# The front of a hybrid encoder layer: keys and values of the attention projected last and kept on chip, queries first

## The chip, the core and the metric

One of the eight cores of a Trainium2 chip runs the kernel. Its engines work side by side and wait for each other by semaphores: PE (TensorE: matmuls and transposes, results into PSUM), DVE (VectorE), ACT (ScalarE), POOL (GpSimd) and SP (SyncE, which here only issues transfers, as POOL does too). The metric is the time of one execution on the device in microseconds (us), the median of several runs.

## What is computed

The layer works on x of 1024 tokens by 1024 channels in fp32. After a LayerNorm one projection of 2048 columns is split into retention (queries, keys, values, gate of 256 each), an S5 branch (256), and windowed attention (512 of queries, 128 of keys, 128 of values). The three results are joined, projected out, added to the residual, normed, and followed by an expert layer of 16 experts and a last norm:

```
proj = jnp.einsum('bld,de->ble', h, w_in[l])
rq, rk, rv, rg, su, aq, ak, av = jnp.split(proj, _split_points(), axis=-1)
...
kb = jnp.concatenate([kp[:, :-2], kp[:, 1:-1], kp[:, 2:]], axis=2)
...
scores = jnp.einsum('bcqkgd,bcskd->bckgqs', qb, kb).astype(f32)
...
scores = scores - slopes * jnp.abs(rel).astype(f32)
...
m = jnp.maximum(jnp.max(scores, axis=-1, keepdims=True), sink_f)
p = jnp.exp(scores - m)
denom = jnp.sum(p, axis=-1, keepdims=True) + jnp.exp(sink_f - m)
probs = (p / denom).astype(v.dtype)
out = jnp.einsum('bckgqs,bcskd->bcqkgd', probs, vb)
...
h = layer_norm(DEEPNORM_ALPHA * h + mix, ln1_g[l], ln1_b[l])
ffn = expert_choice_ffn(h, router_w[l], exp_w_gate[l], exp_w_up[l], exp_w_down[l])
```

Each block of 128 queries sees its own and both neighbouring blocks of keys; eight query heads share two heads of keys and values.

## The kernel before

Products in fp32 are made of three matmuls: each operand is split into a high part (ScalarE copies it) and the remainder (VectorE subtracts), and high x high, low x high and high x low are summed in PSUM (lines 74 to 76). Weights come in pieces of 1 MB as raw tiles (tag wraw, pool raw, two slots; `Units.load`, line 121) and are split half by half into tiles whl (lines 125 and 130).

The program up to about 305 us is `front()`. Its pieces are put with `at(place, fn)` at places, numbers that are sorted once; the program of every engine follows that order. Each engine works its instructions off in order. The string `order` (line 1165) sets the middle of it: K0, K1 and V0, V1 are the halves (512 tokens) of the attention's keys and values, q00 to q31 the four pieces of 128 columns of queries by half, g0 to g7 the gates and r0 to r7 the outputs of the eight chunks of the retention, and o0 to o3 the four output products of S5 (lines 807 and 810). WA holds the weights of keys and values, W6 and W7 those of the queries, WG those of the gate. Between them run the S5 lags (class Lags, lines 718 to 761): matmuls at line 739, copied by ScalarE into a tile KC (lines 749, 751), which lies in the pool raw with tag wraw too, and stored from there by POOL in eight transfers m_d (line 761).

Keys, before: the PSUM rows of a half are split into a tile kst (lines 849 and 858) and stored to DRAM (line 861). Values: they are copied (line 866), turned by four transposes, split into kst and stored (line 887). Queries: kst (lines 851 and 893), stored four times for each piece (q_d, line 899). Near the end of the front, POOL loads KHL (keys, 64 channels of high part twice over and remainders) and AV (values) from DRAM (lines 1294, 1296) into the space of the split weights, and the queries of a step as qs (line 1285; a ring of three).

Attention has 16 steps i, two to a block of 128 tokens. `attention_scores` takes four heads: two matmuls each (lines 1326, 1327), and VectorE adds the bias and takes the maximum while it writes a score row S (line 1329; rows in a ring of 12; the small statistics asm in a ring of 4). `attention_exp` is ScalarE's exponential (line 1345), `attention_out` scales, transposes (line 1364) and multiplies with AV (po, line 1371). From step 2 on the steps stand in a loop in which a scheduler of the tile framework orders the instructions; output projection (lines 74 to 76 with WO), statistics (z, lines 1406 and 1493) and the router run in the same loop, each some steps behind. Ahead of the loop, the front ends with the S5 gate: YG (line 814), transposes (line 822), gate matmuls (line 828), glu and YO (lines 836 to 838), with hb, half of the gate's bias (line 781). The experts follow at about 520 us.

## Time and profile before

| | |
|---|---|
| median of 3 runs | 1681.29 us (1679.31 to 1686.14) |
| the profiled execution | 1684.39 us |
| its span in the profile | 1682.7 us |
| TensorE busy | 1601.5 us (95%) |
| VectorE busy | 1413.9 us (84%) |
| ScalarE busy | 1126.2 us (67%) |
| GpSimd busy | 209.4 us (12%) |

The profile gives times from the span's start. An entry of the timeline is start, duration, engine, line and operation; in brackets stands how long the engine was idle just before, and what ended that. PEclk is the granted clock of TensorE as a share of full speed. Matmuls overlap each other, so their cost is the distance of their starts, not the duration of one.

### The profile page before, as it was taken

How to read it: one execution, taken by the hardware profiler on the slowest of the kernel's cores; microseconds unless marked ns; L12 is line 12 of the kernel's file. 1: busy time of each engine (PE TensorE's matmuls, PEld its weight loads, DVE VectorE, ACT ScalarE, POOL GpSimd, SP SyncE). 2: the span in 40 equal slices, each digit the busy share in tenths (PEclk: the TensorE clock that was granted, in tenths of full speed). 3: DMA queues.
4: the chain of work that ended last, by engine and by line, in shares of the span. 5: the costliest groups of instructions: out<-in, count | busy, mean ns of one | idle time of the engine just before them, and what ended most of it. 6: DMA issues, size and time to landing. Idle time of an engine off the chain costs nothing.

```text
span 1682.7 us, 21145 instructions
## 1 busy us (share of the span) xinstructions
PE 1601.5 (95%) x7704; PEld 1294.4 (77%) x7704; DVE 1413.9 (84%) x1728; ACT 1126.2 (67%) x1266; POOL 209.4 (12%) x243
## 2 busy tenths in 40 slices
PE   6998998799898999999999999999999999999997
PEld 4886887477776788888888888888887787778785
DVE  7984872677788999998988988889888999989996
ACT  4644463666654677777777777777777777877773
POOL 3001211101101010101101011010111213221221
PEclk9998999899999999999999999999999999999998
DMA  4564478714316899999999999999999999999993
GB/s 181 190 165 128 132 206 254 215 49 140 95 63 258 307 386 384 408 379 383 365 392 368 366 398 354 386 374 382 386 364 407 397 395 382 382 410 385 397 418 139
DMA packets 104986, 512.03 MB, mean 304 GB/s; under 512 B 13233, under 2 KB 28337, under 8 KB 54194
## 3 DMA queue, kind: packets, MB, share of 16 engines
q1 hardware_dynamic: 88354, 479.75, 74.7%
q0 software_dynamic: 16528, 30.94, 6.6%
q8 instruction: 60, 0.98, 0.2%
q14 instruction: 44, 0.36, 0.1%
HBM read 464.50 MB, written 46.14 MB: 303 GB/s over the span
## 4 chain that ended last, share of the span: by engine, by line
PE 59%; DVE 16%; DMA 10%; issue 8%; ACT 6%; POOL 1%; SPq 0%; POOLq 0%; DVEq 0%; ACTq 0%
PE gu L1827 26%; PE y L1827 13%; DVE whl L1874 6%; PE mm L74 4%; PE mm L76 4%; PE mm L75 4%; DMA zz<-acc_d 3%; DMA wraw<-in_exp_w_gate 3%; ACT whl L1867 2%; DMA wraw<-in_exp_w_down 2%; PE tp L1812 2%; PE po L1371 1%; ACT S L1345 1%; DMA wraw<-in_exp_w_up 1%; DMA qs<-q_d 1%
## 5 line engine op out<-in xcount | busy, mean ns | idle before, releaser
L1874 DVE TENSOR_TENSOR whl<-wraw,whl 128x2048 fp32r<-128x2048 f32 x384 | 873.3, 2289 | 95.0 <-ACT whl L1867 94.5
L1867 ACT ACTIVATE whl<-wraw 128x2048 fp32r<-128x2048 f32 x384 | 734.6, 1917 | 245.7 <-PE gu L1827 86.7
L1827 PE MATMUL gu<-whl,xT 128*128 128x512 f32 x3072 | 741.0, 398 | 0.0
L1827 PEld LDWEIGHTS gu<-whl,xT 128*128 128x128 f32 x3072 | 571.3, 189 | 124.7
L1827 PE MATMUL y<-whl,hT 128*128 128x512 f32 x1536 | 368.7, 395 | 0.7 <-ACT hT L65 0.7
L1827 PEld LDWEIGHTS y<-whl,hT 128*128 128x128 f32 x1536 | 288.6, 188 | 69.5 <-ACT hT L65 0.9
L1801 POOL DMA_INDIRECT xs<-h_d,index x15 | 41.4, 2758 | 738.5 <-PE y L1827 490.0
L74 PE MATMUL mm<-hT,whl 128*128 128x512 f32 x160 | 65.8, 412 | 0.0
L65 ACT ACTIVATE hT<-tp 128x512 fp32r<-128x512 f32 x80 | 45.9, 583 | 28.7 <-PE tp L1812 14.4
L76 PE MATMUL mm<-hT,whl 128*128 128x512 f32 x160 | 63.0, 394 | 0.0
L75 PE MATMUL mm<-hT,whl 128*128 128x512 f32 x160 | 62.6, 391 | 0.0
L66 DVE TENSOR_TENSOR hT<-tp,hT 128x512 fp32r<-128x512 f32 x80 | 54.1, 684 | 9.2 <-ACT hT L65 9.1
L74 PE MATMUL mm<-WO,yh 128*128 128x512 f32 x128 | 53.2, 415 | 4.7 <-ACT yh L65 4.7
L1812 PE MATMUL tp<-ident,hid 128*128 128x128 f32 x256 | 39.4, 277 | 14.3 <-DVE hid L1909 14.3
L75 PE MATMUL mm<-WO,yh 128*128 128x512 f32 x128 | 52.1, 407 | 0.0
L1812 PEld LDWEIGHTS tp<-ident,hid 128*128 128x128 f32 x256 | 31.3, 141 | 25.9 <-DVE hid L1909 18.8
L1329 DVE CUSTOM_DVE_ANT_0 S<-at,R,sink 128x384 f32<-128x384 f32 (+1 forms) x64 | 35.8, 581 | 17.3 <-PE tp L1364 11.7
L76 PE MATMUL mm<-WO,yl 128*128 128x512 f32 x128 | 50.3, 403 | 0.0
L74 PE MATMUL mm<-whl,hT 128*128 128x512 f32 (+1 forms) x128 | 46.8, 366 | 1.5 <-ACT hT L65 1.4
L1345 ACT ACTIVATE S<-S,asm 128x384 f32<-128x384 f32 (+1 forms) x64 | 36.9, 577 | 14.1 <-DVE asm L1332 13.9
L76 PE MATMUL mm<-whl,hT 128*128 128x512 f32 (+1 forms) x128 | 44.4, 347 | 1.2 <-DVE hT L66 1.2
L75 PE MATMUL mm<-whl,hT 128*128 128x512 f32 (+1 forms) x128 | 44.4, 347 | 1.1 <-DVE whl L130 1.1
(430 smaller groups left out, 1792.3 us busy)
## 6 DMA issues: line engine op xcount, KB each, us to landing
wraw<-in_exp_w_gate SPq DMA_DIRECT2D x128, 1024.0 KB, 7.7
wraw<-in_exp_w_up SPq DMA_DIRECT2D x128, 1024.0 KB, 8.1
wraw<-in_exp_w_down SPq DMA_DIRECT2D x128, 1024.0 KB, 8.0
wraw<-in_w_in SPq DMA_DIRECT2D x8, 1024.0 KB, 7.2
x<-in_x SPq DMA_DIRECT2D x8, 512.0 KB, 4.6
h_d<-x SPq DMA_DIRECT2D x8, 512.0 KB, 3.2
q_d<-kst SPq DMA_DIRECT2D x32, 128.0 KB, 4.8
wraw<-in_w_out SPq DMA_DIRECT2D x4, 1024.0 KB, 6.4
```

The source lines that it names most:

```text
L65: nc.scalar.activation(hi, src, AF.Copy)
L66: eng.tensor_tensor(lo, src, hi.bitcast(F32), OP.subtract)
L74: nc.tensor.matmul(ps, a[0], b[0], start=start, stop=False)
L75: nc.tensor.matmul(ps, a[0], b[1], start=False, stop=False)
L76: nc.tensor.matmul(ps, a[1], b[0], start=False, stop=stop)
L1329: nc.vector.tensor_tensor_reduce(s[:, :W], ps[:, :W], K.R[:, ro:ro + W], 2.0 ** -(h + 1), K.sink[:, h:h + 1], OP.add, OP.max, accum_out=m[ ...
L1345: nc.scalar.activation(S[g][:, :W], S[g][:, :W], AF.Exp, bias=nm[:, g:g + 1], accum_out=rs[:, g:g + 1])
L1801: nc.gpsimd.indirect_dma_start(out=xs, out_offset=None, in_=K.h1_dram, in_offset=bass.IndirectOffsetOnAxis(ap=K.index[:, e:e + 1], axis=0))
L1812: K.nc.tensor.transpose(pt[:, c, :], src[:, (c0 + c) * P:(c0 + c + 1) * P], K.ident)
L1827: nc.tensor.matmul(ps, a[s][c], u[:, t, i * w:(i + 1) * w], start=first and id(ps) not in began, stop=last and left[id(ps)] == 0)
L1867: self.K.nc.scalar.activation(u[:, 0, :], self.raw[k1].rearrange("p a b -> p (a b)"), AF.Copy)
L1874: self.K.nc.vector.tensor_tensor(u[:, 1, :], raw, u[:, 0, :].bitcast(F32), OP.subtract)
```

## The change

Queries are projected first and keys and values last: the string `order` is new, W6 takes the early load of WA, W7 is loaded next and WA last. Keys and values are not stored to DRAM and loaded again: their PSUM rows are split where they lie into the tiles KHL and AV, for keys in pieces of 64 rows, with two copies for the second 64 rows. That takes out eight stores and four loads of keys and two and two of values.

For the space, the pool of split weights becomes two pools. The one of side 1 is closed when the retention is done (`keys_space`), and KHL and AV are put there. The last two tiles of side 0 become the score rows (`attention_space`), ten in place of twelve; the statistics asm come from another pool, three in place of four.

The scores of steps 0 and 1 are issued ahead of and among the S5 gate instead of behind it. At the start of the kernel, the small chain `ops[0:14]` (rsmall) moves ahead of the second norm, the split of WK[1] behind it, and the second part of the first projection to a later place. The diff, cut to its core:

```diff
-        u = self.K.hl.tile([P, 2, 1024], F32R, name="whl", tag=f"whl{self.side}", bufs=2)
+        u = self.K.hl[self.side].tile([P, 2, 1024], F32R, name="whl", tag="whl", bufs=2)
...
-def key_rows(K, parts, half):
-
-    ks = parts[0]
-    K.nc.vector.tensor_tensor(ks[:, 1], parts[1].ps, ks[:, 0].bitcast(F32), OP.subtract)
+def key_rows(K, p, half):
+
+    nc, hs = K.nc, slice(half * 512, (half + 1) * 512)
+    a, b = slice(0, 64), slice(64, P)
     for kv in range(2):
-        for r in range(2):
-            K.nc.sync.dma_start(K.k_dram[half][kv][r * 64:(r + 1) * 64], ks[kv * 64:(kv + 1) * 64].bitcast(F32))
+        split(K, K.KHL[kv][a, 0, hs], K.KHL[kv][a, 1, hs], p.ps[kv * 64:(kv + 1) * 64])
+    for kv in range(2):
+        nc.scalar.activation(K.KHL[kv][b, 0, hs], K.KHL[kv][a, 0, hs].bitcast(F32), AF.Copy)
+        nc.vector.tensor_copy(K.KHL[kv][b, 1, hs], K.KHL[kv][a, 1, hs].bitcast(F32))
...
-def value_high(K, pt):
-    vs = K.ast.tile([P, 4, 2, 2, 64], F32R, name="kst", tag="k4", bufs=3)
...
-def value_parts(K, parts, half):
-    vs, pt = parts
-    K.nc.vector.tensor_tensor(vs[:, :, :, 1], pt, vs[:, :, :, 0].bitcast(F32), OP.subtract)
-    K.nc.sync.dma_start(K.v_dram[half], vs.bitcast(F32))
+def value_parts(K, pt, half):
+    av = K.AV[:, half * 4:half * 4 + 4]
+    split(K, av[:, :, :, 0], av[:, :, :, 1], pt.rearrange("p b (k c) -> p b k c", k=2))
...
+    spread(9.95, 0.001, ops[0:5])
...
-    at(10.3, lambda: WK[1].high(0))
-    at(10.4, lambda: WK[1].high(1))
-    at(10.5, lambda: WK[1].low(0))
-    at(10.6, lambda: WK[1].low(1))
+    spread(10.3, 0.01, ops[5:14])
     at(11.0, norm[1].gain)
     at(11.1, norm[1].shift)
-    spread(11.2, 0.001, ops[0:5])
-    spread(11.3, 0.01, ops[5:14])
+    at(11.2, lambda: WK[1].high(0))
+    at(11.3, lambda: WK[1].high(1))
+    at(11.4, lambda: WK[1].low(0))
+    at(11.5, lambda: WK[1].low(1))
...
-        at(s + 6.2 if t else 11.8, lambda p=p, c=6 if t else 4: p.part(c, 8))
+        at(s + 6.2, lambda p=p, c=6 if t else 4: p.part(c, 8))
...
-    at(B + 2.0, WA.load)
+    at(B + 2.0, W6.load)
...
-    order = "K0 g0 g1 K1 r0 V0 r1 g2 r2 g3 V1 r3 q00 g4 r4 g5 q10 r5 g6 r6 q01 g7 r7 q11 q20 q30 o0 o1 q21 o2 q31 o3".split()
+    order = "q00 g0 g1 q01 r0 q10 r1 g2 r2 g3 q11 r3 q20 g4 r4 g5 q21 r5 g6 r6 q30 g7 r7 q31 V0 o0 K0 o1 V1 o2 K1 o3".split()
...
-    at(E0 + 1.5, lambda: WA.high(0))
+    at(E0 + 1.5, lambda: W6.high(0))
...
-    for wt, place, prev in ((W6, V0 + 4, ("K1", "V1")), (W7, V0 + 21, ("q01", "q11"))):
+    for wt, place, prev in ((W7, V0 + 15, (("q01", 0), ("q11", 1))), (WA, V0 + 21, (("q21", 1), ("q31", 0)))):
         at(place, wt.load)
...
-    at(R, lambda: close(X["retB"][0], K.c_ret))
+
+    def keys_space():
+        close(X["retB"][0], K.c_ret, K.c_hl1)
+        X["kv"] = pool("kv", side="right")
+        K.KHL = [X["kv"][1].tile([P, 2, L], F32R, name=f"KHL{kv}") for kv in range(2)]
+        K.AV = X["kv"][1].tile([P, NT, 2, 2, 64], F32R, name="AV")
+    at(R, keys_space)
...
-    def keys():
-        close(K.c_hl)
-        X["kv"] = pool("kv", side="right")
-        K.kv = X["kv"][1]
-        attention_keys(K)
-        X["at2"] = pool("at2", side="right")
-        K.at2 = X["at2"][1]
-    at(where["q31"] + 5.7, keys)
...
-        at(where["q21"] + 6.0 + i * 0.1, lambda i=i: attention_queries(K, i))
+        at(where["K1"] + 1.0 + i * 0.1, lambda i=i: attention_queries(K, i))
+    at(where["K1"] + 5.7, lambda: attention_space(K))
     for i in range(2):
-        at(G + 10.3 + i * 2.6, lambda i=i: attention_scores(K, i))
-        at(G + 12.9 + i * 2.6, lambda i=i: attention_exp(K, i))
+        at(G - 0.2 + i * 1.1, lambda i=i: attention_scores(K, i))
+        at(G + 10.4 + i * 2.6, lambda i=i: attention_exp(K, i))
...
+def attention_space(K):
+
+    t = [K.hl[0].tile([P, 2, 1024], F32, name="S", tag="whl", bufs=2).rearrange("p a b -> p (a b)") for _ in range(2)]
+    K.score = [t[i // 5][:, i % 5 * 3 * P:(i % 5 + 1) * 3 * P] for i in range(10)]
+    K.heads = 0
...
-    sm = K.at2.tile([P, 6, 4], F32, name="asm", bufs=4)
+    sm = K.small.tile([P, 5, 4], F32, name="asm", bufs=3)
...
-        s = K.at2.tile([P, 3 * P], F32, name="S", bufs=12)
+        s = K.score[K.heads % 10]
+        K.heads += 1
```

Three places of the program, in the order of each engine. First ScalarE, at the second KC of the S5 lags (at is the PSUM tile it copies, QT and qfb are retention's queries, kst the first projected piece of keys before, of queries after). Before:

```order
L340 ACTIVATE QT_165<-mm_1481 128x512
L751 ACTIVATE KC_1509<-at_1537 16x4x112 [waits PE_49]
L751 ACTIVATE KC_1509<-at_1571 16x4x112 [waits PE_49]
L749 ACTIVATE KC_1633<-at_1616 16x4x128 [waits DMASW3_49,DMASW2_49,DMASW4_49,DMASW1_49,DMASW5_49,DMASW0_49,DMASW6_49,DVE_49,DMASW7_49,PE_49,Activation_49]
L370 ACTIVATE qfb_1635<-QT_165 64x2x128 [waits DMAHW3_49]
L370 ACTIVATE qfb_1635<-QT_165 64x2x128 x3
L849 ACTIVATE kst_1661<-mm_1553 128x512 [waits DMAHW3_49,DMAHW4_49,DMAHW2_49,DMAHW5_49,DMAHW1_49,DMAHW7_49,DMAHW0_49,PE_49]
```

After:

```order
L340 ACTIVATE QT_162<-mm_1478 128x512
L751 ACTIVATE KC_1506<-at_1534 16x4x112 [waits PE_49]
L751 ACTIVATE KC_1506<-at_1568 16x4x112 [waits PE_49]
L749 ACTIVATE KC_1628<-at_1613 16x4x128 [waits DVE_49,PE_49,Activation_49]
L370 ACTIVATE qfb_1630<-QT_162 64x2x128 [waits DMAHW3_49]
L370 ACTIVATE qfb_1630<-QT_162 64x2x128 x3
L848 ACTIVATE kst_1656<-mm_1550,qscale_1327 128x512 [waits DMAHW3_49,DMAHW2_49,DMAHW4_49,DMAHW1_49,DMAHW5_49,DMAHW0_49,DMAHW7_49,PE_49,Pool_49]
```

The order of these rows is the same, but the second KC no longer waits for the transfers issued by POOL (DMASW). Beside it, SP's queue in the same stretch. Before, the load of a raw tile (wraw, W6) stood ahead of the stores of the first piece:

```order
L731 DMA BX_1629<-bx_d01_82 128x64 [waits DMAHW0_49,DVE_49]
L121 DMA wraw_1631<-in_w_in 128x2048 [waits Activation_49]
L861 DMA k_d00_103<-kst_1661 64x1024 [waits DMAHW1_49,DVE_49,Activation_49]
L861 DMA k_d00_103<-kst_1661 64x1024 [waits DMAHW2_49]
L861 DMA k_d01_104<-kst_1661 64x1024 [waits DMAHW3_49]
L861 DMA k_d01_104<-kst_1661 64x1024 [waits DMAHW4_49]
```

After, with the loads of retention's states (kv) behind those stores:

```order
L890 DMA q_d0_0_75<-kst_1656 64x512 [waits DMAHW2_49]
L890 DMA q_d0_0_75<-kst_1656 64x512 [waits DMAHW3_49]
L351 DMA kv_1698<-kv_d1_96 128x512 [waits DMAHW4_49]
L351 DMA kv_1793<-kv_d2_97 128x512 [waits DMAHW5_49]
L121 DMA wraw_1796<-in_w_in 128x2048 [waits DMASW5_49,DMASW4_49,DMASW6_49,DMASW3_49,DMASW7_49,DMASW2_49,DMAHW6_49,DMASW1_49,DMASW0_49]
L890 DMA q_d1_0_77<-kst_1819 64x512 [waits DMAHW7_49,Activation_49]
```

W6's load is gone from here, and W7's load, behind the first stores and two loads of kv, now has the wait for the transfers that POOL issued. The second place is VectorE at hb, at the end of the retention (whl is the last split weight, WO the output projection's). Before:

```order
L893 SCALAR_TENSOR_TENSOR kst_2780<-mm_2725,qscale_1330,kst_2780 128x512 [waits DMAHW4_49,Activation_49]
L130 TENSOR_TENSOR whl_2782<-wraw_1877,whl_2782 128x1024 [waits PE_49,Activation_49]
L781 TENSOR_SCALAR hb_2836<-bg_2834 128x2 [waits DMAHW2_49,DMAHW3_49,DMAHW1_49,DMAHW5_49,DVE_49,DMAHW6_49,PE_49,Activation_49]
L893 SCALAR_TENSOR_TENSOR kst_2821<-mm_2760,qscale_1330,kst_2821 128x512 [waits DMAHW7_49,DMAHW0_49]
L893 SCALAR_TENSOR_TENSOR kst_2880<-mm_2811,qscale_1330,kst_2880 128x512 [waits DMAHW6_49,DMAHW5_49,DMAHW7_49,DMAHW4_49,Activation_49]
L66 TENSOR_TENSOR WO1_2911<-wraw_2573,WO0_2910 128x1024 [waits PE_49,Activation_49]
L66 TENSOR_TENSOR WO1_2911<-wraw_2573,WO0_2910 128x1024 [waits Activation_49]
```

After:

```order
L884 SCALAR_TENSOR_TENSOR kst_2769<-mm_2714,qscale_1327,kst_2769 128x512 [waits DMAHW2_49,Activation_49]
L130 TENSOR_TENSOR whl_2771<-wraw_1874,whl_2771 128x1024 [waits PE_49,Activation_49]
L781 TENSOR_SCALAR hb_2835<-bg_2833 128x2 [waits DMAHW1_49,DMAHW3_49,DMAHW0_49,DMAHW4_49,DVE_49,DMAHW7_49,PE_49,Activation_49]
L66 TENSOR_TENSOR AV_2826<-tp_2846,AV_2826 128x8x64 [waits Activation_49]
L66 TENSOR_TENSOR KHL0_2824<-mm_2863,KHL0_2824 64x512 [waits Activation_49]
L66 TENSOR_TENSOR KHL1_2825<-mm_2863,KHL1_2825 64x512 [waits Activation_49]
L860 CAST KHL0_2824<-KHL0_2824 64x512 [waits DVE_49]
L860 CAST KHL1_2825<-KHL1_2825 64x512 [waits DVE_49]
```

The rows of queries behind hb are gone, and splits into AV and KHL stand there. The third place is TensorE behind the last S5 output (o3). Before, with the first scores behind all sixteen gate matmuls:

```order
L822 MATMUL tp_3055<-ident_128,YG_2831 128x128 x3
L822 MATMUL tp_3061<-ident_128,YG_2831 128x128 [waits PE_49]
L822 MATMUL tp_3061<-ident_128,YG_2831 128x128 x3
L828 MATMUL mm_3073<-yT_2984,wg_2832 128x512 [waits DVE_49]
L828 MATMUL mm_3073<-yT_2984,wg_2832 128x512 [waits Activation_49]
L828 MATMUL mm_3081<-yT_2984,wg_2832 128x512 [waits PE_49]
L828 MATMUL mm_3081<-yT_2984,wg_2832 128x512
L828 MATMUL mm_3092<-yT_2984,wg_2832 128x512 [waits Activation_49]
L828 MATMUL mm_3092<-yT_2984,wg_2832 128x512
L828 MATMUL mm_3099<-yT_2984,wg_2832 128x512 [waits Activation_49]
L828 MATMUL mm_3099<-yT_2984,wg_2832 128x512
L1326 MATMUL at_3107<-KHL0_3037,qs_2962 128x256 [waits DMASW3_49,DMASW0_49]
```

After:

```order
L1310 MATMUL at_3052<-KHL0_2824,qs_2979 128x256 [waits DVE_49]
L1311 MATMUL at_3052<-KHL0_2824,qs_2979 128x256
L1310 MATMUL at_3056<-KHL0_2824,qs_2979 128x256 [waits DVE_49]
L1311 MATMUL at_3056<-KHL0_2824,qs_2979 128x256
L822 MATMUL tp_3062<-ident_122,YG_2830 128x128 [waits Activation_49]
L822 MATMUL tp_3062<-ident_122,YG_2830 128x128 x3
L822 MATMUL tp_3068<-ident_122,YG_2830 128x128 [waits PE_49]
L822 MATMUL tp_3068<-ident_122,YG_2830 128x128 x3
L1310 MATMUL at_3075<-KHL1_2825,qs_2981 128x256 [waits DMASW1_49,DVE_49]
L1311 MATMUL at_3075<-KHL1_2825,qs_2981 128x256
```

The scores (at, line 1310) of step 0 now stand ahead of the transposes of YG, and those of step 1 between them and the gate.

## Rows read from the trace of the kernel before

**Rows 1.** Busy time of the engines (with the number of instructions) in three stretches: the S5 output, the head of attention, the experts; then the granted clock of TensorE, the DMA engines' share, GB/s.

```profile
250.00:291.00 41.00, 36.47 (x206) 32.13 (x205) 9.73 (x11) 12.69 (x18) 3.90 (x6) 0.92 0.85 257
291.00:346.00 55.00, 41.94 (x155) 28.89 (x156) 34.77 (x96) 38.05 (x93) 6.65 (x15) 0.84 0.63 189
...
700.00:1682.00 982.00, 959.90 (x4374) 776.12 (x4372) 876.19 (x578) 721.38 (x529) 129.88 (x77) 0.99 0.96 375
```

**Rows 2.** Waits of TensorE from 0 to 305 us, by line and releaser: total in us, times, the longest.

```profile
PE at L739 <- ACT KC L749: 6.6, 1, 6.6
...
PE mm L807 <- DVE kst L893: 4.5, 1, 4.5
PE tp L173 <- DVE x L164: 4.1, 2, 2.6
```

**Rows 3.** The same from 291 to 540 us.

```profile
PE at L1326 <- DMA qs<-q_d: 5.3, 1, 5.3
PE mm L74 <- ACT yh L65: 4.7, 3, 3.5
```

**Rows 4.** Timeline of all engines from 148 to 167 us, at the two KC tiles: start, duration, engine, line.

```profile
149.55 0.42 SPq L121 DMA_DIRECT2D wraw<-in_w_in  x1
...
149.86 4.50 POOL L761 DMA_DIRECT2D m_d<-KC  x8 [22.99 <-DVE stmp L314]
...
150.04 1.05 PE L739 MATMUL at<-WO,BX 128*16 128x128 f32 x8
...
151.01 0.39 PE L74 MATMUL mm<-whl,hT 128*128 128x256 f32 x1
...
152.38 0.28 PE L76 MATMUL mm<-whl,hT 128*128 128x256 f32 x1
...
158.64 0.59 ACT L749 ACTIVATE KC<-at 16x512 f32<-16x512 f32 x1 [12.81 <-DMA m_d<-KC]
...
159.28 1.89 PE L739 MATMUL at<-WO,BX 128*16 128x128 f32 x8 [6.62 <-ACT KC L749]
...
161.10 0.58 PE L74 MATMUL mm<-whl,hT 128*128 128x256 f32 x1
...
163.96 1.77 PE L739 MATMUL at<-WO,BX 128*16 128x128 f32 x8
```

**Rows 5.** Timeline of ScalarE and of SP behind it, at the second split weight and the loads of kv; and from the list of transfers, the loads of the input weights (number, size, us from issue to landing).

```profile
175.69 1.06 ACT L125 ACTIVATE whl<-wraw 128x1024 fp32r<-128x1024 f32 x1
...
183.24 1.29 ACT L416 ACTIVATE ro<-po,rnm,rrs 128x64 f32<-128x64 f32 x4 [4.74 <-DVE rnm L413]
...
166.36 2.32 SPq L351 DMA_DIRECT2D kv<-kv_d  x2
...
wraw<-in_w_in SPq DMA_DIRECT2D x8, 1024.0 KB, 7.2
```

**Rows 6.** Timeline of TensorE in the start, at the transposes of the second token tile.

```profile
22.42 1.07 PE L173 MATMUL tp<-ident,x 128*128 128x128 f32 x8 [0.98 <-DVE rsmall L259]
```

**Rows 7.** Timeline of SP, VectorE and TensorE from 261 to 290 us, the S5 output products.

```profile
261.36 0.43 SPq L777 DMA_DIRECT2D bg<-in_ssm_b_glu  x1
...
264.21 0.17 DVE L781 TENSOR_SCALAR hb<-bg 128x2 f32<-128x2 f32 x1 [9.77 <-DMA bg<-in_ssm_b_glu]
...
265.13 0.80 PE L807 MATMUL mm<-MU 128*128 128x128 f32 x2 [4.51 <-DVE kst L893]
...
266.57 0.64 PE L807 MATMUL mm<-MU 128*128 128x128 f32 x2
...
267.85 0.64 PE L807 MATMUL mm<-MU 128*128 128x128 f32 x2
...
288.80 0.39 PE L807 MATMUL mm<-MU 128*128 128x128 f32 x2
...
289.47 0.39 PE L807 MATMUL mm<-MU 128*128 128x128 f32 x2
```

**Rows 8.** Instructions by line and shape up to 520 us, splits of 64 and of 128 rows: busy time, mean ns of one, idle time ahead.

```profile
L66 DVE TENSOR_TENSOR yl<-po,yh 64x512 fp32r<-64x512 f32 x16 | 10.9, 680 | 4.2 <-ACT yh L65 3.9
...
L65 ACT ACTIVATE yh<-po 64x512 fp32r<-64x512 f32 x16 | 9.4, 587 | 7.5 <-PE po L1371 7.3
...
L858 DVE TENSOR_TENSOR kst<-mm,kst 128x512 fp32r<-128x512 f32 x2 | 1.4, 676 | 0.0
```

**Rows 9.** Timeline of all engines from the last S5 output to the first statistic.

```profile
291.01 0.60 ACT L814 ACTIVATE YG<-mm 128x512 f32<-128x512 f32 x1 [1.99 <-PE mm L810]
...
305.04 0.39 PE L1326 MATMUL at<-KHL,qs 128*128 128x256 f32 x1 [4.15 <-DVE asm L1329]
...
309.31 0.78 POOL L1285 DMA_DIRECT2D qs<-q_d  x1 [1.15 <-PE at L1327]
...
320.85 0.66 PE L1326 MATMUL at<-KHL,qs 128*128 128x384 f32 x1 [5.31 <-DMA qs<-q_d]
...
346.24 0.69 DVE L1406 SCALAR_TENSOR_TENSOR z<-z,mm 128x512 f32<-128x512 f32 x1 [1.40 <-PE mm L76]
```

**Rows 10.** The last statistic's line (eight times, one to a token tile; durations, first and last start), and by shape, up to 520 us, the instruction of a score row on VectorE and the exponential of a row of 256 on ScalarE.

```profile
L1493 DVE SCALAR_TENSOR_TENSOR z<-z,l1mv,g x8: 1264/1284/1285, 370.4 to 519.6; 128x1024 f32<-128x1024 f32 x8
...
L1329 DVE CUSTOM_DVE_ANT_0 S<-at,R,sink 128x384 f32<-128x384 f32 x48 | 28.4, 614 | 16.1 <-PE tp L1364 11.7 <-PE at L1327 3.9 <-ACT S L1358 0.2
...
L1345 ACT ACTIVATE S<-S,asm 128x256 f32<-128x256 f32 x16 | 7.9, 495 | 0.2 <-DVE asm L1332 0.2
```

More of the change, by code (lines that the diff above doesn't have):

```diff
@@ L2182, in build @@
     K.kv_dram = [dr.tile([P, 2, 256], F32, name=f"kv_d{t}") for t in range(NT)]
-    K.k_dram = [[dr.tile([P, 2, 512], F32, name=f"k_d{t}{k}") for k in range(2)] for t in range(2)]
-    K.v_dram = [dr.tile([P, 4, 2, 2, 64], F32, name=f"v_d{t}") for t in range(2)]
     K.u_dram = dr.tile([P, 2, 8, P], F32, name="u_d")
@@ L2199, in build @@
     c_hy, K.hy = pool("hy", bufs=4)
-    K.c_hl, K.hl = pool("hl", bufs=4, side="right")
+    hl = [pool(f"hl{i}", bufs=2, side="right") for i in range(2)]
+    K.hl = [x[1] for x in hl]
+    c_hl0, K.c_hl1 = (x[0] for x in hl)
     _, K.s5small = c_s5s = pool("s5small")
```

55 lines of the change are left out of this document (19 added, 36 removed).

## The prediction

> **What bounds the kernel now.** I read the time stretch by stretch first [rows 1]. From 700 to 1682 us, in the experts, TensorE is busy 959.9 of 982 us at granted clock 0.99 with the DMA engines at 0.96: that part has a fixed length and starts when the layer ahead of it is done, so what the front saves should reach the end one for one. The change touches only the front and the attention loop, up to 520 us. Then the waits of TensorE in that part, longest in total [rows 2, 3]: 6.6 us on ScalarE's KC, 5.3 us on a qs load, 4.7 us on yh, 4.5 us on a kst row, 4.1 us on x. The reader is to see that these are single waits, not a pattern, and that the longest are followed by TensorE at half its clock (1.2 GHz, the lower of its two levels; the granted clock of 291 to 346 is 0.84).
>
> The sum is made against the profiled execution, 1684.4 us (span 1682.7, 1.7 around it); the median of the runs is 1681.3, so 3.1 us are taken off at the end.
>
> **The KC wait goes: 9.4 us, of which 1 is paid back.** KC is a tile of the pool of raw weights, which has two slots. Before, W6's load at 149.55 takes a slot between the two KC tiles, so the second KC falls on the slot of the first, whose eight m_d stores start only at 149.86. ScalarE waits 12.81 us for them, until 158.64, and TensorE 6.62 us, until 159.28 [rows 4]. Now W6 was loaded long before, the two KC take the two slots, and the row of the second waits for no DMA; the wait on m_d passes to W7's load, on SP's queue. Half clock behind the idle time: 12 matmuls of 256 columns take 2.86 us from 161.10 to 163.96, against 1.5 at full rate (11 starts in 1.37 us from 151.01 to 152.38), and the two groups of eight 1.89 and 1.77 against 1.05. That is 1.3 + 0.84 + 0.72 = 2.8 us, so 6.6 + 2.8 = 9.4. What is late next: W7's load stands behind q00's four stores and two kv loads, where before k_d's stores and the same kv loads end at 168.7 [rows 5]. These follow the kst of the first unit, some 7 us earlier now: issue at about 161.7, landing 7.2 us later at 168.9. ScalarE wants W7 behind the next kst, before at 175.69, now at about 166.3: it would stand for up to 2.6 us, with the qfb copies of the next chunk queued behind it. Later on it idles 4.74 us before 183.24, which covers most of that. I take 1 us, range 0 to 2.6.
>
> **Start and retention: 1.8 us.** The chain of rsmall moves ahead of WK1's splits and ahead of the second norm, and WK1 behind that norm; at 22.42 TensorE had waited 0.98 us there [rows 6]. I take 0.9, with 0 and 2 as ends (the x waits are 4.1 in all [rows 2]). V's transposes and ScalarE's and VectorE's V and K work leave the stretch in which TensorE never idles. The two groups of four transposes are worth 0.9 us there, but they come back in the next stretch and are counted in its term.
>
> **The S5 output stretch: 2.5 us, from -1 to 4.** VectorE's hb waits until 264.21 for a load issued at 261.36, and the kst row behind it holds the PSUM buffer that the first S5 output (o0) needs: TensorE idles 4.51 us, until 265.13 [rows 7]. Then a group of six matmuls takes 1.28 us (266.57 to 267.85) against 0.67 (288.80 to 289.47), for some 4.3 groups: 2.6 us. In all 7.1. Now V0 and then o0 and K0 stand there; o0's buffer was freed by a kst row ahead of hb and V0's is read by ScalarE, so hb holds only the splits behind it. o0 (2.7), four transposes (0.45) and K0 (5.5) run meanwhile. o1 then waits for the states' load (Z), which SP issues behind the same y_d store: I put 3 us of idle time and 0.7 of half clock there, and 0.9 for the moved transposes. 7.1 - 4.6 = 2.5.
>
> K's path itself: a 128-row split in two instructions becomes, for each half, eight of 64 rows. A 64x512 piece costs 0.587 us on ScalarE and 0.680 on VectorE [rows 8], and a 128x512 one takes no less (0.676), so ScalarE gets about 3.5 us more and VectorE 4.1 in all. They lie at 250 to 291, where ScalarE is busy 12.7 of 41 us and VectorE 9.7 [rows 1]: I cost them at nothing. If that cover were gone they would cost the 4.1 at most. The Trainium skill (Perfetto Trace Analysis, Optimizing Scalar/DVE Operations) asks for grouped, larger operations, since each has a fixed overhead; this change does the reverse, and if the pieces stood on the path the sum would be 4.1 us smaller. The same section holds against it only where the engine is saturated, and rows 1 show that it is not.
>
> The 16 transfers that go (eight stores and four loads of keys, two and two of values) gave up no visible wait of their own; I cost their removal at nothing, though less DMA beside the Z and qs loads can only help.
>
> **The head of attention: 6 us, from 0 to 9.** Before, from YG of the last S5 output at 291.01 to the first z at 346.24 are 55.2 us, with TensorE busy 41.9 of 55 at granted clock 0.84 [rows 1, 9]: it waits 4.15 us at 305.04 while VectorE works through glu and YO before the first scores, and 5.31 us at 320.85 for a qs load whose buffer had come free late (the load at 309.31). Now the scores of steps 0 and 1 are issued ahead of and among the gates, so VectorE does them first and the qs buffers come free 10 to 20 us earlier: the 5.31 and the half clock behind it go. What is late next: the exponentials still stand behind glu on ScalarE (its table load comes once), and steps 2 and 3 need rows of a ring that now holds ten, so TensorE runs dry at some 14.6 us from that point and waits for the first probabilities until about 24.5, ten us at one stretch. I get these by stepping through the rows of the new order with the durations of before: scores 0, transposes and scores 1 to 6.3, the gates with scores 2 among them to 14.6; on ScalarE the last glu to 16.6, the table load, eight exponentials of 0.5 us with their sums [rows 10] and the first products. From there on the order is that of before, and the first z comes at about 49 us instead of 55.2. That is 6.
>
> **The loop: 3 us, from -5 to 7.** The eight rows of the last statistic run from 370.4 to 519.6, 21.3 us a tile [rows 10]. One wait stands out, 3.5 us on yh [rows 3], where eight exponentials of two steps stood ahead of it on ScalarE. In the new order I find no such pair ahead of an odd step's output. Half of it and its half clock, 3 us, is a guess between those ends.
>
> Sum: 9.4 - 1 + 0.9 + 0.9 + 2.5 + 6 + 3 = 21.7. 1684.4 - 21.7 = 1662.7, and against the median 1681.3 - 21.7 = 1659.6: **1660**, from 1649 (every term near its better end) to 1667 (every term but KC near half).
>
> **Rivals.** *Given back at the head of attention*: the wait for qs is replaced by the wait for the first probabilities, Z takes as long as hb did, and the loop gains nothing; 10.2 us of the first two terms remain: 1671, from 1667 to 1677. For it: ScalarE's glu and table load are not moved, and ten us of idle time will be followed by half clock, as the shorter ones of before were. Against: the qs load is ready.
>
> *The ring slows the loop, and it ends slower*: ten rows instead of twelve and three small tiles instead of four let TensorE run 2.5 steps ahead instead of 3. The last two scores of a step then wait for the transposes of the step two before. If every one of 14 steps pays a bubble of two scores on VectorE, 2 x 0.614 = 1.2 us [rows 10], and 1 more in half clock, that is 14 x 2.2 = 31 us against 18.7 gained outside the loop: 1681.3 + 12 = 1693, from 1684. It decides when a tile takes 18.7 / 7 = 2.7 us more than 21.3, over 24. For it: the loop has bubbles already. Against: 2.5 steps are 25 us of TensorE's work, and one step's chain of scores, exponentials, products and transposes is about 10. The Trainium skill (Perfetto Trace Analysis, Identifying Performance Opportunities) says that repeated bubbles on the engine that should be full can mean too little space for the next tile; by that rule the smaller ring is the wrong way and this rival holds. The trace of before has no bubble that repeats each step.
>
> *The KC wait stays*, since W7's load now waits for m_d on SP and everything behind it on SP with it (q01's stores, kv): 8 of the 9.4 are lost, 1668.
>
> **How the numbers follow.** The forecast 0.62 (1649 to 1667), given back 0.20, slower loop 0.06, KC stays 0.07, and 0.05 for a better loop below 1649. Half a per cent, 8.4 us, is about what a measurement of this kernel tells from no change: under 1672.9 is faster. That is the forecast, the KC rival, the better loop and half of the second: 0.84. Same 0.10, slower 0.06. The range leaves out the slower loop and the ends: 1648 to 1675.
>
> **What would show it.** The second KC on ScalarE without a DMA wait and TensorE at full clock from 150 to 170; W7's split at about 167 with a wait under 3 us; o0 directly behind V0 and one wait of about 3 us on Z at o1; the first z 49 us behind the last S5 output, and no wait on qs; tiles of the loop at 21 us or less. It would be wrong if a wait of over 5 us appears on SP behind W7's load, if the first z comes no earlier than 55 us behind the last S5 output, or if tiles take over 24 us.

## The result, and the profile after

| | before | after |
|---|---|---|
| median | 1683.22 us (1679.31 to 1686.14, 4 runs) | 1661.07 us (1658.70 to 1666.00, 4 runs) |
| profiled execution, span | 1684.39, 1682.7 us | 1658.70, 1657.0 us |

The ratio is 0.987, with a 95% interval of 0.984 to 0.991: faster, by 22.2 us or 1.3%. To see where, I take places that both programs have and subtract their times in the two profiled executions (us); these two lie 25.7 us apart, so the table adds up to more than the medians:

| stretch | before | after | difference | forecast |
|---|---|---|---|---|
| start to the first store of m_d | 149.86 | 148.59 | -1.3 | -0.9 |
| to the last group of eight at line 739 (KC) | 14.1 | 5.3 | -8.8 | -9.4 |
| to the last transpose of ro (retention) | 89.4 | 88.2 | -1.2 | +0.1 (W7 +1, -0.9) |
| to the last S5 output product | 37.0 | 38.2 | +1.2 | -2.5 |
| to the first z (head of attention) | 55.9 | 43.9 | -12.0 | -6 |
| to the first gate product of an expert (loop) | 177.4 | 174.9 | -2.5 | -3 |
| to the end (experts) | 1159.1 | 1157.9 | -1.2 | 0 |

The experts start 24.5 us earlier and keep their length, as [rows 1] let expect: TensorE is busy 955.47 of their last 977 us. Two stretches of the kernel after, columns as in [rows 1], the first of them that of KC:

```profile
145.00:175.00 30.00, 30.00 (x197) 24.76 (x195) 27.60 (x74) 13.13 (x27) 9.91 (x17) 1.00 0.79 175
...
680.00:1657.00 977.00, 955.47 (x4362) 772.47 (x4360) 873.32 (x576) 718.66 (x527) 132.46 (x77) 1.00 0.97 376
```

From 145 to 175 us TensorE has no idle time and a granted clock of 1.00. The stretch in which K is split, from the last transposes of ro to the last YG, before and after:

```profile
253.35:291.01 37.66, 33.12 (x185) 29.21 (x183) 8.84 (x10) 10.97 (x15) 3.91 (x6) 0.91 0.83 250
```

```profile
242.16:281.42 39.26, 33.53 (x197) 29.77 (x195) 11.11 (x16) 15.39 (x23) 1.50 (x2) 0.91 0.67 205
```

ScalarE has 4.4 us more than before, VectorE 2.3, and neither is half full. TensorE's waits, from 0 to 300 us:

```profile
PE mm L810 <- DMA Z<-s_d: 5.7, 1, 5.7
PE tp L173 <- DVE x L164: 5.3, 2, 3.2
```

and from 265 to 515 us:

```profile
PE tp L1349 <- ACT S L1343: 7.8, 1, 7.8
PE mm L74 <- ACT yh L65: 3.5, 4, 1.4
```

The waits for KC, for the kst row, for qs and the single long one for yh [rows 2, 3] are gone. New are one for Z, and one for the first probabilities (S). The timeline at the two KC tiles (to be read against [rows 4, 5]):

```profile
147.34 0.59 ACT L749 ACTIVATE KC<-at 16x512 f32<-16x512 f32 x1 [2.77 <-PE at L739]
...
148.59 4.51 POOL L761 DMA_DIRECT2D m_d<-KC  x8 [22.86 <-DVE stmp L314]
...
149.90 0.69 ACT L848 ACTIVATE kst<-mm,qscale 128x512 fp32r<-128x512 f32 x1 [0.40 <-issue]
150.49 0.57 ACT L749 ACTIVATE KC<-at 16x512 f32<-16x512 f32 x1
...
153.92 1.05 PE L739 MATMUL at<-WO,BX 128*16 128x128 f32 x8
...
158.56 0.33 SPq L121 DMA_DIRECT2D wraw<-in_w_in  x1
...
165.78 1.06 ACT L125 ACTIVATE whl<-wraw 128x1024 fp32r<-128x1024 f32 x1 [0.59 <-DMA wraw<-in_w_in]
```

ScalarE begins the second KC at 147.34 instead of 158.64 and waits there only for the matmuls whose result it copies; the row at 150.49 is the next one of the same KC. The group of eight takes 1.05 us instead of 1.77. W7's load is issued 7.2 us ahead of its split, which holds ScalarE for 0.59 us. The S5 output, against [rows 7]:

```profile
244.86 0.33 SPq L431 DMA_DIRECT2D y_d<-roT  x1
...
250.09 0.33 SPq L775 DMA_DIRECT2D wg<-in_ssm_w_glu  x1
...
252.84 1.93 SPq L799 DMA_DIRECT2D Z<-s_d  x4
...
253.28 0.17 DVE L781 TENSOR_SCALAR hb<-bg 128x2 f32<-128x2 f32 x1 [10.04 <-ACT KHL L65]
...
258.50 1.27 PE L810 MATMUL mm<-W,Z 128*128 128x128 f32 x4 [5.72 <-DMA Z<-s_d]
259.56 0.64 PE L807 MATMUL mm<-MU 128*128 128x128 f32 x2
...
260.84 0.63 PE L807 MATMUL mm<-MU 128*128 128x128 f32 x2
...
280.32 0.61 PE L810 MATMUL mm<-W,Z 128*128 128x128 f32 x4
```

TensorE waits for nothing behind hb now. But Z's loads are issued 2.75 us behind wg, with five issues between them, and all of these stand behind the store y_d until 250.09. TensorE idles 5.72 us, and the next full groups of six take 1.28 us each (259.56 to 260.84), at a granted clock of 0.50 from 258.5 to 262.5. The head of attention, against [rows 9]:

```profile
280.98 0.75 DVE L860 CAST KHL<-KHL 64x512 fp32r<-64x512 f32 x2
...
281.42 0.60 ACT L814 ACTIVATE YG<-mm 128x512 f32<-128x512 f32 x1
...
282.31 0.39 PE L1310 MATMUL at<-KHL,qs 128*128 128x256 f32 x1 [0.90 <-DVE asm L1314]
...
283.52 0.74 POOL L1273 DMA_DIRECT2D qs<-q_d  x1 [10.44 <-PE at L1311]
...
286.14 0.74 POOL L1273 DMA_DIRECT2D qs<-q_d  x1 [1.88 <-PE at L1311]
...
295.23 0.69 ACT L836 ACTIVATE glu<-mm,hb 128x512 f32<-128x512 f32 x1 [2.82 <-DVE YO L838]
295.94 1.28 ACT L1328 ACT_TABLE_LOAD   x1
...
301.91 1.97 PE L1349 MATMUL tp<-ident,S 128*128 128x128 f32 x8 [7.81 <-ACT S L1343]
...
324.22 0.69 DVE L1391 SCALAR_TENSOR_TENSOR z<-z,mm 128x512 f32<-128x512 f32 x1 [1.08 <-PE mm L76]
```

TensorE runs dry 12.7 us behind YG and waits until 20.5 us for S, which stands behind the last glu and the table load on ScalarE. The first z comes 42.8 us behind YG (55.2 before). The tiles of the loop, by the last statistic, take 21.0 us (21.3 before).

### The profile page after: what moved, and what is told of

It reads as the page before. It is cut to its first block, busy times and chain, and to the rows that moved or that the text cites. A ratio compares the mean times of both kernels' runs of the same rounds, so it can differ in the third digit from the quotient of the medians.

```text
span 1657.0 us, 21108 instructions
## 1 busy us (share of the span) xinstructions
PE 1587.8 (96%) x7704; PEld 1288.8 (78%) x7704; DVE 1416.3 (85%) x1734; ACT 1129.3 (68%) x1272; POOL 211.4 (13%) x237
## 4 chain that ended last, share of the span: by engine, by line
PE 60%; DVE 15%; DMA 9%; issue 7%; ACT 7%; POOL 1%; SPq 0%; POOLq 0%; DVEq 0%; ACTq 0%
PE gu L1812 27%; PE y L1812 14%; DVE whl L1859 6%; DMA zz<-acc_d 4%; PE mm L74 4%; PE mm L76 4%; PE mm L75 4%; ACT whl L1852 3%; DMA wraw<-in_exp_w_down 2%; PE tp L1797 2%; DMA wraw<-in_exp_w_gate 1%; PE po L1356 1%; ACT S L1330 1%; DVE pT L66 1%; PE sm L1456 1%
## 5 line engine op out<-in xcount | busy, mean ns | idle before, releaser
L1797 PE MATMUL tp<-ident,hid 128*128 128x128 f32 x256 | 39.7, 279 | 13.5 <-DVE hid L1894 13.4
L75 PE MATMUL mm<-WO,yh 128*128 128x512 f32 x128 | 50.9, 398 | 0.0
L1894 DVE TENSOR_TENSOR hid<-hid,gu 128x512 f32<-128x512 f32 x64 | 43.6, 681 | 1.9 <-PE gu L1812 1.9
```

What stands on the lines that cost most here:

```text
L75: nc.tensor.matmul(ps, a[0], b[1], start=False, stop=False)
L1797: K.nc.tensor.transpose(pt[:, c, :], src[:, (c0 + c) * P:(c0 + c + 1) * P], K.ident)
L1894: at(self.after, q, 3, lambda: nc.vector.tensor_tensor(self.h[q], self.h[q], self.pg[q][1], OP.mult))
```

## The experiments

Each ratio is against the kernel before on the same chip, with its 95% interval. Where "behind" or "ahead" is said of a place, the profiled executions are compared.

**e1_w6_late and e5_kc_shared: the KC wait alone, taken out of the kernel before.** Two ways that leave the string `order` and the ring as they were: W6's load behind the second KC, or both KC tiles in one raw tile.

```diff
-    for wt, place, prev in ((W6, V0 + 4, ("K1", "V1")), (W7, V0 + 21, ("q01", "q11"))):
+    for wt, place, prev in ((W6, V0 + 15, ("K1", "V1")), (W7, V0 + 21, ("q01", "q11"))):
```

```diff
-            self.kc = K.raw.tile([P, 8, 15, 16], F32, name="KC", tag="wraw")[0:16]
+            if g2 == 0:
+                self.both = K.raw.tile([P, 8, 15, 16], F32, name="KC", tag="wraw")
+            self.kc = self.both[g2 * 32:g2 * 32 + 16]
...
-        dg = K.ast.tile([P, 8, 16], F32, name="dg", tag="q2", bufs=3)[0:16]
+        dg = K.ast.tile([P, 8, 16], F32, name="dg", tag="q2", bufs=3)[g2 * 32:g2 * 32 + 16]
```

> The kernel before with one number changed: W6's load at place V0 + 15 instead of V0 + 4, so that no raw tile comes between the two KC tiles. Theory (the slot rotation made the KC wait): the second KC on ScalarE waits for no DMA, TensorE's 6.6 us wait at line 739 is gone and the half clock behind it too, the second group of lags ends 8 to 9 us earlier, and the whole is 7 to 9 us faster than before (ratio about 0.995). Rival (the wait is m_d's length itself or the DMA load of that stretch): the wait stays above 4 us and the time within 3 us of before. Second rival (gain given back): the retention waits for W6's load, which now comes late, and less than 4 us reach the end.

> The kernel before with both KC tiles in one raw tile (the second on partitions 32 to 47), so that the second needs no slot; W6's load keeps its early place. It differs from the run with W6 loaded late in that W6 is there in time. Theory (that run lost 5 us in the retention because V's path on ScalarE waited for W6, and 5 us because the loop was ordered otherwise): the KC wait is gone, the last transposes of ro come 8.5 to 9.5 us earlier than before, and so does the first z; how much of it reaches the experts depends on the order that the scheduler finds for the loop, within 6 us. Rival (the retention has a bound of its own that takes the gain back): the last ro comes less than 6 us earlier.

Measured: e1 1683.96 us against 1679.38, ratio 1.002 (1.000 to 1.004); e5 1679.34 against 1684.21, 0.996 (0.994 to 0.998). In both the KC wait is gone: the last group at line 739 comes at 154.66 and 155.35 instead of 163.96. So the slot made the wait. In e1 half of the gain is paid back at once, because W6 then comes late (SP, then ScalarE):

```profile
161.90 0.91 SPq L121 DMA_DIRECT2D wraw<-in_w_in  x1
...
170.84 1.06 ACT L125 ACTIVATE whl<-wraw 128x1024 fp32r<-128x1024 f32 x1 [5.04 <-DMA wraw<-in_w_in]
```

so that the retention ends 4.7 us earlier than before, in e5 9.2. And in both the attention loop takes 182.8 us instead of 177.4, though no line of it was touched: the framework's scheduler put it in another order (two heads of step 4 ahead of the first output projection, where before had one). In that order TensorE idles some 16 us of the loop instead of 12.4, at a granted clock of 0.96 instead of 0.98. So the KC term is 9 us where it arises (e5), but at the start of the experts nothing is left of it in e1 and 2.7 us in e5; neither run gained the 7 to 9 us that I had expected of e1. Why the scheduler changed the order is not shown.

**e2_w7_early: the KC wait put back into the changed kernel.** W7's load ahead of the second KC, as W6's was before.

```diff
-    for wt, place, prev in ((W7, V0 + 15, (("q01", 0), ("q11", 1))), (WA, V0 + 21, (("q21", 1), ("q31", 0)))):
+    for wt, place, prev in ((W7, V0 + 4, (("q01", 0), ("q11", 1))), (WA, V0 + 21, (("q21", 1), ("q31", 0)))):
```

> The changed kernel with one number changed: W7's load at V0 + 4 instead of V0 + 15, between the two KC tiles as W6's was before. Theory: the KC wait on ScalarE is back at 11 to 13 us, TensorE waits 6 to 7 us at line 739 and runs at half clock behind it, and the time is 7 to 9 us above the changed kernel. Rival (the new order of queries first removed the wait): no wait, time within 3 us of the changed kernel.

Measured: 1670.96 us against 1679.38, 0.994 (0.991 to 0.996). Timeline of ScalarE:

```profile
157.65 0.59 ACT L749 ACTIVATE KC<-at 16x512 f32<-16x512 f32 x1 [12.74 <-DMA m_d<-KC]
```

The wait of [rows 4] is back. The group at line 739 is 9.05 us later than in the changed kernel, 8.7 of them behind the first store of m_d; the experts start 9.1 us later, the loop is the same (174.9 us), and the ratio is 0.006 above that of the changed kernel, some 10 us. That is the term, alone, with the order behind it unchanged.

**e3_scores_late: the scores of steps 0 and 1 back behind the gate**, in the changed kernel.

```diff
-        at(G - 0.2 + i * 1.1, lambda i=i: attention_scores(K, i))
-        at(G + 10.4 + i * 2.6, lambda i=i: attention_exp(K, i))
+        at(G + 10.3 + i * 2.6, lambda i=i: attention_scores(K, i))
+        at(G + 12.9 + i * 2.6, lambda i=i: attention_exp(K, i))
```

> The changed kernel with scores and exponentials of steps 0 and 1 at their old places (G + 10.3 and G + 12.9, 2.6 apart), keys and values still on chip. Theory (early scores free the qs buffers and get VectorE's work out of the way): the wait on qs or the wait behind glu and YO returns, first z 6 to 12 us later than in the changed kernel measured from the last S5 output, time 6 to 12 us above it. Rival (the head gained because the loads of keys and values no longer take the DMA engines beside the qs loads): a qs load lands in 4 to 5 us instead of 11, the first z comes at most 3 us later, and the time is within 3 us of the changed kernel.

Measured: 1663.05 us against 1679.38, 0.989 (0.984 to 0.994). TensorE's waits from 265 to 515 us:

```profile
PE at L1310 <- DVE asm L1314: 5.8, 7, 4.4
```

The wait of 4.15 us on VectorE [rows 9] is back as 4.4, the head takes 49.4 us instead of 43.9, and the experts start 4.75 us later. Medians and ratios show only 2 to 3 us of it, with intervals that overlap, where I had expected 6 to 12. But no wait for qs came back, although the scores stand where they stood before and a qs load takes 10.4 us to land, with no keys and values to load beside it. So the early scores are worth 5.5 us of the head in the profile, and the qs wait stays away without them.

**e6_ring10_before and e7_ring12_after: the ring of score rows alone**, ten rows in the kernel before, twelve in the changed kernel (two more tiles beside KHL).

```diff
-        s = K.at2.tile([P, 3 * P], F32, name="S", bufs=12)
+        s = K.at2.tile([P, 3 * P], F32, name="S", bufs=10)
```

```diff
+        K.more = [X["kv"][1].tile([P, 3 * P], F32, name=f"S{i}") for i in range(2)]
...
-    K.score = [t[i // 5][:, i % 5 * 3 * P:(i % 5 + 1) * 3 * P] for i in range(10)]
+    K.score = [t[i // 5][:, i % 5 * 3 * P:(i % 5 + 1) * 3 * P] for i in range(10)] + K.more
...
-        s = K.score[K.heads % 10]
+        s = K.score[K.heads % 12]
```

> The kernel before with the ring of score rows at ten instead of twelve, nothing else. Theory (the wait of 5.3 us on qs came from the scheduler placing the first scores of step 4 ahead of the first output projection, which a ring of ten does not let it do): no wait over 2 us on qs, the first z 5 to 7 us earlier after the last S5 output, about 49 to 51 us, as in the run with late scores. Rival (the keys' and values' loads made the qs load late): the wait stays at 4 us or more. Second rival (a smaller ring slows the loop): from the first z to the first expert matmul it takes over 5 us more than the 177.4 of before.

> The changed kernel with two more score rows beside KHL and AV, a ring of twelve. If the smaller ring cost the changed kernel anything, the loop from the first z to the first expert matmul is shorter than its 174.9 by 3 us or more and the time lower. If the ring's size only chooses between orders, the time is within 4 us either way; the scores of step 4 then stand ahead of the first output projection again, but their qs load was issued ten us ahead, so no wait on qs over 1 us.

Measured: e6 1674.68 us against 1684.21, 0.994 (0.992 to 0.996); e7 1673.56 against 1684.21, 0.993 (0.990 to 0.996), by the ratio 9 us above the changed kernel and with the experts starting 14.3 us later. In e6 the KC wait stays (6.8 us), the head takes 49.4 us instead of 55.9 and the loop 175.1 instead of 177.4. What happened to the qs wait, on POOL and then on TensorE in e6:

```profile
307.61 0.78 POOL L1285 DMA_DIRECT2D qs<-q_d  x1 [1.16 <-PE at L1327]
```

```profile
314.25 0.44 PE L1326 MATMUL at<-KHL,qs 128*128 128x384 f32 x1 [0.47 <-DVE asm L1329]
...
314.71 0.40 PE L74 MATMUL mm<-WO,yh 128*128 128x512 f32 x1
```

This load takes 10.7 us to land, as long as the one of [rows 9] (11.4 us), so it was not made faster. But in the program's order 15 heads of scores stand ahead of the first output projection on TensorE with ten rows, none beyond step 3; with twelve there are 17, and the seventeenth, the first of step 4, waits for this load with the projection queued behind it [rows 9, 320.85]. In e7 19 heads stand ahead of it; there the scores are early, the load comes in time and no wait for qs is left. But TensorE waits elsewhere, as here before transposes, and e7 is slower by more than the 4 us that I had allowed either way:

```profile
324.21 0.66 PE L1350 MATMUL tp<-ident,S 128*128 128x128 f32 x4 [3.18 <-DVE pT L66]
```

With e3, the head of attention is now known for both rings and both places of the scores (us):

| | scores late | scores early |
|---|---|---|
| twelve rows | 55.9 (before) | 50.9 (e7) |
| ten rows | 49.4 (e6, e3) | 43.9 (after) |

Early scores give 5.0 or 5.5 us, ten rows 6.5 or 7.0, each with or without the other (single executions, and a head of unchanged code differs by up to 1.6 us). The wait for qs stands in one corner only, so either edit alone takes it away; and since ten rows gain as much where it is already gone, it is not the whole of what the ring costs. e6 and e3 agree although e3 has the rest of the change and three small tiles asm, which therefore do not show in the head. Ten rows do not always keep step 4 back: in e10 below, 17 heads stand ahead of the projection.

**e9_ring8_after, e11_ring9_after and e12_ring11_after: the size of the ring** in the changed kernel: `K.heads % 8`, `% 9`, `% 11`, with as many rows in the list (for eleven, one tile beside KHL).

> The changed kernel with a ring of eight score rows, four to a tile. So far rings of twelve took 177 to 183 us from the first z to the first expert matmul and rings of ten 173 to 175. Theory (a smaller ring keeps the scheduler from placing scores far ahead of the output projection, and the loop does not need them): the loop takes 172 to 176 us and the time is within 4 us of the changed kernel. Rival (the ring is a latency bound, as the prediction's slower case has it, and ten was just enough): with eight rows a step's scores wait for the transposes of the step two before in every step, TensorE waits on VectorE or ScalarE in each tile, the loop takes over 185 us and the time is 10 us or more above the changed kernel.

> The changed kernel with a ring of nine score rows. Rings so far: twelve 181.4 us and ten 174.9 from the first z to the first expert matmul, eight 184.5 (changed kernel). If the ring were a bound by latency below and by order above, nine lies between: 176 to 182 us. If each size only draws another order, nine may come out anywhere from 173 to 185, and TensorE's waits for score rows do not grow in step with it.

> The changed kernel with a ring of eleven score rows (one beside KHL and AV). If the size works steadily, eleven lies between ten and twelve: 175 to 181 us from the first z to the first expert matmul, and the time between 1661 and 1674. If each size draws another order, it may come out above twelve or below ten.

| rows | median, us | ratio | head, us | loop, us |
|---|---|---|---|---|
| 8 (e9) | 1672.97 | 0.994 (0.991 to 0.996) | 45.1 | 184.5 |
| 9 (e11) | 1665.14 | 0.990 (0.988 to 0.993) | 45.2 | 177.3 |
| 10 (after) | 1661.07 | 0.987 (0.984 to 0.991) | 43.9 | 174.9 |
| 11 (e12) | 1664.43 | 0.989 (0.985 to 0.993) | 45.8 | 176.9 |
| 12 (e7) | 1673.56 | 0.993 (0.990 to 0.996) | 50.9 | 181.4 |

Ten is the lowest of the five. The losses at eight and twelve are clear in the loop (6.5 us and more); nine and eleven lie 2.0 to 2.4 us from ten there, and their intervals overlap with its. The loop's row of the windows (columns as in [rows 1]), of the changed kernel:

```profile
324.20:499.10 174.90, 163.92 (x886) 132.83 (x886) 138.38 (x361) 107.21 (x257) 21.72 (x54) 1.00 0.30 98
```

with eight rows:

```profile
324.70:509.20 184.50, 169.29 (x896) 136.26 (x895) 141.30 (x368) 109.15 (x263) 22.17 (x55) 0.97 0.30 95
```

and with twelve:

```profile
332.00:513.40 181.40, 166.99 (x878) 136.18 (x877) 135.43 (x349) 102.72 (x242) 21.72 (x53) 0.96 0.29 93
```

The idle time of TensorE (length less busy time) is 11.0, 15.2 and 14.4 us, and its busy time, for about the same matmuls, 163.9, 169.3 and 167.0, at granted clocks of 1.00, 0.97 and 0.96. So eight and twelve lose 3.4 to 4.2 us by more waits and 3 to 5 by a slower clock. Waits for the rows themselves would be VectorE's score instruction waiting for the transposes that free a row. With nine rows it does so for 6.1 us in four waits; with eight the profile shows none in the loop. That too few rows cause the loss at eight is therefore not shown.

**e8_old_start: the start of before** in the changed kernel (one execution).

```diff
-    spread(9.95, 0.001, ops[0:5])
...
-    spread(10.3, 0.01, ops[5:14])
+    at(10.3, lambda: WK[1].high(0))
+    at(10.4, lambda: WK[1].high(1))
+    at(10.5, lambda: WK[1].low(0))
+    at(10.6, lambda: WK[1].low(1))
...
+    spread(11.2, 0.001, ops[0:5])
+    spread(11.3, 0.01, ops[5:14])
...
-        at(s + 6.2, lambda p=p, c=6 if t else 4: p.part(c, 8))
+        at(s + 6.2 if t else 11.8, lambda p=p, c=6 if t else 4: p.part(c, 8))
```

> The changed kernel with the start of before (rsmall, the split of WK1 and the second part of the first projection at their old places). The first m_d store of the lags came 1.3 us earlier in the changed kernel than before. Theory: that is the start's, and here it comes at 149.9 again, 1.3 us later. Rival: it is from the order behind the start, and the store stays at 148.6.

Measured: 1663.1 us, and the first store of m_d at 149.94 instead of 148.59, 1.35 us later. But 0.5 of that is the first load of all, of x, for which TensorE waits; e8, then the changed kernel:

```profile
5.23 3.75 PE L935 MATMUL mm<-x,ones 1*128 1x512 f32 x4 [5.23 <-DMA x<-in_ln_in_b]
```

```profile
4.73 3.75 PE L935 MATMUL mm<-x,ones 1*128 1x512 f32 x4 [4.73 <-DMA x<-in_ln_in_b]
```

From this matmul to the store it is 144.71 us in e8 and 143.86 in the changed kernel, and the other runs bear it out: 144.7 in e1, e5 and e6, which have the old start, 143.9 to 144.0 in those with the new one. The new start is worth 0.8 us. Of the 3.7 us at the first expert the rest is mainly a Z wait that came out 0.5 longer and a head that took 45.5.

**e4_z_first and e10_z_first_lows_late: what was late next, taken away.** e4 issues the states Z ahead of MU and W. e10 does that too, and moves the two remainders of the last piece of WO, on VectorE, behind the scores and the gate (line numbers of e10 differ a little).

```diff
-    at(O + 0.01, lambda: out.load(*qs[2], X["s5o"][1], 1))
-    at(O + 0.02, lambda: out.states(*qs[1], X["s5o"][1]))
+    at(O + 0.02, lambda: out.load(*qs[2], X["s5o"][1], 1))
+    at(O + 0.01, lambda: out.states(*qs[1], X["s5o"][1]))
```

```diff
+            hi = K.WO[0][c // 4][:, c % 4 + i, :]
+            K.nc.scalar.activation(hi, self.raw[c][:, i, :], AF.Copy)
+        if c < 6:
+            self.lows(c)
...
     at(G + 5.0, lambda: mat.parts(6))
+    at(G + 10.2, lambda: mat.lows(6))
```

> The changed kernel with the states' load of the second S5 output (Z) issued ahead of the load of MU and W of the third, the two exchanged on SP. Theory: o1's wait of 5.7 us on Z is set by the place of Z's load in SP's queue; it shrinks by about 1.9 us, the distance of the two issues, and the half clock behind it stays; 1.5 to 2.5 us faster than the changed kernel. Rival: the wait is set by the transfers' length and only changes by under 1 us, or o2 then waits for MU and W as long as o1 gained.

> The changed kernel with Z's load ahead as in the earlier run, and VectorE's two remainders of the last piece of the output weights moved behind the scores and glu (ScalarE's part stays). Theory (the wait of 7.8 us for the first probabilities is the chain glu, YO on VectorE, last glu on ScalarE, table load, exponentials, and the two remainders of 1.2 us each stand in it): the last glu starts about 2.4 us earlier after the last S5 output, the wait on ScalarE's S falls to 5 to 6 us, and the first z comes 1.5 to 2.5 us earlier after it than the 45.5 of the run with Z first; the whole is 3 to 5 us faster than the changed kernel. Rival (the chain is set by ScalarE alone): the wait stays at 7 us or more.

Measured: e4 1659.06 us against 1679.38, 0.987 (0.982 to 0.992); e10 1654.37 against 1683.50, 0.983 (0.979 to 0.987). The timeline of SP and TensorE in e4:

```profile
251.47 0.90 SPq L799 DMA_DIRECT2D Z<-s_d  x2
...
255.41 0.95 PE L810 MATMUL mm<-W,Z 128*128 128x128 f32 x4 [2.36 <-DMA Z<-s_d]
```

Z is issued 1.4 us earlier, the wait falls from 5.72 to 2.36, the S5 output ends 3.2 us earlier and the experts start 2.5 earlier. The two transfers also land in 3.8 us (median), where they took 5.5 behind MU and W, so that the wait shrinks by more than the 1.9 us expected. Medians and ratios do not tell e4 from the changed kernel. The timeline of e10:

```profile
291.16 0.69 ACT L836 ACTIVATE glu<-mm,hb 128x512 f32<-128x512 f32 x1 [1.38 <-PE mm L828]
...
297.84 1.97 PE L1358 MATMUL tp<-ident,S 128*128 128x128 f32 x8 [6.37 <-ACT S L1352]
```

The last glu no longer waits for VectorE (2.82 us on YO in the changed kernel), the wait for S falls from 7.81 to 6.37, the head from 43.9 to 41.9, and the experts start at 494.15, 5.0 us earlier than in the changed kernel. This is the fastest version, and the wait for S ended between what I had expected (5 to 6 us) and the rival (7 or more); its interval still overlaps with the changed kernel's.

## Why the prediction was right, and where it was not

The number held, 1661 against 1660, and so did the sign. That it is so close is partly luck. The S5 output came out 3.7 us worse than its term, the head of attention 6 better and the retention 1.3, which cancels in part; and in the profiled executions, against which the sum was made, the gain was 25.7 us, not 21.7.

**KC: right in mechanism and size.** From the first store of m_d to the last group of eight it is 8.8 us less in the changed kernel and in e5, and e2 puts 8.7 back. The payback at W7 was 0.59 us of wait, within 0 to 2.6. I had moved the kst of the first unit 7 us ahead, by TensorE's wait; but it stands behind the second KC on ScalarE, which had waited 12.81, and came at 149.90 instead of 160.83, 10.9 us earlier. So W7's load was issued at 158.56, 3.1 us earlier than I had it.

**Start: right in size.** 0.8 us by e8 and by the other runs, counted from the first matmul, against 0.9; another 0.5 of the 1.3 in the table is a first wait for x that was longer in the profile of before (2.57 us, 2.1 to 2.2 in the other runs). The wait of 0.98 on rsmall is gone, but one of 3.2 on x stands ahead of the second tile now (the two on x are 5.3 in all, 4.1 before), and later ones are gone in its place.

**S5 output: the term with the wrong sign.** hb and the kst row stopped mattering, as foreseen, and the wait on Z came at o1, as foreseen. The step that failed is "I put 3 us of idle time and 0.7 of half clock there". The wait was 5.72 us, and the half clock behind it cost 2.0 more: from 258.50 to the end of the four groups it is 4.46 us, 2.46 at 0.67 a group. I had put Z behind the store y_d, but not behind the six issues that stand between: e4 puts Z ahead of four of them and has 3.2 us back.

**K's splits in pieces of 64 rows: nearly hidden.** Between the same two places ScalarE and VectorE took 4.4 and 2.3 us more, and TensorE waited there for Z alone. But the last two copies of keys (VectorE, 280.98) end only as the first score row begins, at 281.77, and TensorE waits 0.90 us for score rows at 282.31: up to 0.9 us of their cost shows, where I had put it at nothing. That the removed transfers of keys and values cost and gave nothing was not tried by itself.

**Head of attention: 12 us instead of 6.** Two steps were off. The wait of 10 us foreseen for the first probabilities came as 7.81, at 12.7 to 20.5 us instead of 14.6 to 24.5: the last glu ends at 14.5, not 16.6, and the way to the probabilities was 4.0 us too long in the stepping. The other 2.2 lie behind, where "from there on the order is that of before" did not hold: 16 heads of scores stand ahead of the first output projection, not 17. And the reason was half of it. "The qs buffers come free 10 to 20 us earlier: the 5.31 and the half clock behind it go" describes something that happens (the loads are issued 2.1 and 4.7 us behind YG, before 15.5 and 18.3), and with twelve rows it is enough (e7). But the wait stays away with late scores too (e3), and with ten rows in the kernel before (e6): it needs a late load and an order that puts a head of step 4 ahead of the first output projection. The sum gave the ring of ten no gain at all; it is worth 6.5 us of the head (e6), the early scores 5.5 (e3), 12.0 together.

**Loop: 2.5 against a guess of 3.** It too comes with the ring: e6 has 2.2 of it on the kernel before.

**The rivals.** *The ring slows the loop* was the wrong way round at this size: ten rows instead of twelve gain 8.7 us from the last S5 output to the first expert in e6, and twelve instead of ten lose 13.5 in e7. Two rows further down a loss does come: with eight the loop takes 184.5 us, 7.1 more than before, or 0.9 us a tile, still short of the 2.7 from which it would have decided; but the waits for rows from which the rival made it are not in that profile. The rule of the Trainium skill that I had named beside this rival (Perfetto Trace Analysis, Identifying Performance Opportunities: repeated bubbles can mean too little space) would have had the step from twelve to ten the wrong way round; whether the loss at eight is of its kind is not shown. *Given back at the head* did not happen, although its wait (7.81 us for S) did; *the KC wait stays* is refuted by the second KC at 147.34 and the 0.59 us at W7.

Left open: why twelve rows give the scheduler a worse order inside the loop, and eight another. I can show the waits and the clock, not the rule by which it chose.
